# GpSimd left with the gathers alone, one-hot rows gated per token on VectorE, and a queue mark moved with each weighing

## The chip, the core and the metric

The kernel runs on one core of a Trainium2 chip. The time is the device time of one execution in microseconds (us), from the first instruction to the last, with the launch around it. Three runs of the kernel before gave 4369.52, 4371.93 and 4373.88 us; the median is 4371.93 us.

A core has five engines that run side by side, each with a queue of its own that is worked off strictly in order: PE (TensorE, matrix products), DVE (VectorE, elementwise and reductions), ACT (ScalarE, activations), POOL (GpSimd) and SP (SyncE, which here only issues DMA transfers). An instruction that waits for another engine holds up everything behind it in its own queue.

## The reference, cut to what matters

The network is a token mixer on 512 tokens, a PEER layer, and two transformer blocks with sparse attention and an MLP. The change lies in the PEER layer (`peer_ffn`), a mixture of 16384 tiny experts:

```python
q = einsum('pd,de->pe', tb, wq).reshape(-1, 8, 2, 128)
s = einsum('phik,hink->phin', q, subkeys)            # 8 heads, 2 halves, 128 keys
s1, i1 = top_k(s[:, :, 0], 16); s2, i2 = top_k(s[:, :, 1], 16)
cand = s1[..., :, None] + s2[..., None, :]           # 16 x 16 candidates
top_s, pos = top_k(cand, 16)
idx  = take_along_axis(i1 * 128 + i2, pos)           # 128 experts per token
gate = softmax(top_s)
act  = gelu(einsum('pd,phkd->phk', tb, table_u[idx]))
out  = einsum('phk,phkd->pd', gate * act, table_v[idx])
```

Each of the 512 tokens picks 128 experts (8 heads times 16), takes a dot product with a row of `peer_u` for each, and sums rows of `peer_v` weighted by gate times activation.

## The kernel before, in words

Everything is float32. A product is made of three matmuls (`mm3`, L160 to L162) on a high and a low part of each operand; `split` (L136, L137) makes the parts, the high one with a copy on ACT and the low one with a subtraction, on DVE unless another engine is named.

The first 128 tokens take the **sparse** way (`peer_few`): for each of the 128 slots a GpSimd indirect DMA (L1371) gathers one row of 1024 numbers of `peer_u` for every token into a buffer `row` (four of them), and DVE takes the dot product with the tokens (`dot`, at most three behind the gather). Then the same with `peer_v` (`axpy`). That makes 256 gathers of 512 KB.

The other 384 tokens take the **dense** way: all 16384 experts are computed, in 32 groups of 512, and a matrix of gates that is mostly zero picks what counts. The work runs in these stages:

- **Route** (`peer_route`): sixteen blocks of queries, with top-16 searches on DVE; for thirteen of them the low part of the weights is made on GpSimd (the last argument on L1166). Then, for each block of 128 tokens, **gates** (`peer_gates`): the second search, and the lookup of the chosen keys by comparing with an index row (`eq`), a multiplication on GpSimd (L1228) and a sum on DVE (L1229). Three transposes of the result on PE (L1241) end a block.
- **Spread** (`peer_spread`): for 96 quads of tokens two sets of one-hot rows are built, 128 wide each: `two` (which second key) and `one` (which first key, times the gate). GpSimd subtracts (L1259), DVE compares (L1260, L1261), PE multiplies the two (L1264), ACT copies the product to `gt`, and the gates go to DRAM (`g_dram`).
- Beside both runs `spill`: PE computes the activations of the first 18 groups (`NSPILL`) ahead of time, and SP stores them in DRAM (`a_dram`). How often it moves is set by ticks in `peer_route` and by `SR` in the spread. The sparse way moves by `FR`: 0.4 of a gather per tick of the last three gates blocks, 0.05 per quad.
- **Rounds**: for 31 groups `prepare` loads the gates and the stored activations of the next group and weighs them (`peer_weigh`: a DVE product L1312, then the split), while `peer_out` loads 2 MB of `peer_v`, splits it (`wl`, L137) and multiplies (72 matmuls of 512 columns per group on the first 17, summed in PSUM). The sparse way moves three gathers per round in the first 17 rounds and twelve after them (`QUOTA`).

The order on each engine is laid down when the program is built: a scheduler issues what it takes to be ready first. `queued(mark, ...)` only adds that an instruction on DVE may not be issued before the marked one. Every `dot` and `axpy` is queued behind `s.mark`. In route and spread the mark moves with each split of a table (L1294); in the rounds it moves where a sum is drained (L1347, L1349), and that happens first at group 16.

Of the kernel before, what the change touches and what calls it, by code (L numbers as in the profile page):

```python
# [15 lines left out]
OP = mybir.AluOpType  # L16
# [27 lines left out]
QN = (6, 5)  # L44
QUOTA = (3, 12)
YR = (0.3, 1.75)
FR = (0.4, 0.05)
SR = 0.67
FL = 3
GB = 2  # L50
# [50 lines left out]
class K:  # L101
# [1030 lines left out]
    def peer_route(s, tk, u2):  # L1132

        nc, I = s.nc, s.I
        skT = tk.tile([128, 16, 128], F32, name="skT")
        sk = I["peer_subkeys"][0].rearrange("h i n k -> n (h i) k")
        for a in range(2):
            wf = s.wp.tile([128, 1024], F32, name="wf", bufs=s.wfb)  # L1140
            f = wf.rearrange("p (a k) -> p a k", a=8)
            nc.sync.dma_start(f, sk[:, 8 * a:8 * a + 8])
            for b in range(2):
                p = s.ps()
                for c in range(4):
                    nc.tensor.transpose(p[:, 128 * c:128 * c + 128], f[:, 4 * b + c], s.ident)
                nc.scalar.activation(skT[:, 8 * a + 4 * b:8 * a + 4 * b + 4].rearrange("p a n -> p (a n)"), p, AF.Copy)
        iota = tk.tile([128, 16], F32, name="iota")
        nc.sync.dma_start(iota, s.C["iota"][:, :16])
        due = [0.0]  # L1150

        def tick(us, what=0):

            due[0] += us * YR[what > 0]
            while due[0] >= 1:
                due[0] -= 1
                yield what
        tv = s.x[:, 1].rearrange("p (b h i k) -> p b h i k", b=4, h=8, i=2)
        ti = tk.tile([128, 4, 8, 2, 16], U32, name="ti")
        lead = s.lin_lead([(I["peer_wq"][0], 0, hh) for hh in range(3)], u2, ("mm",) * 3)  # L1160
        for hh in range(16):
            if hh < 3:
                p = lead[hh]
            else:
                p = s.ps(kind="mm")
                s.lin_acc(I["peer_wq"][0], 0, hh, u2, p, nc.gpsimd)  # L1166
            q = tk.tile([128, T], F32, name="q", bufs=2)
            nc.scalar.activation(q, p, AF.Copy)
            p = s.ps()
            for tb in range(4):  # L1170
                nc.tensor.matmul(p[:, 128 * tb:128 * tb + 128], q[:, 128 * tb:128 * tb + 128], skT[:, hh], start=True, stop=True)
            sc = tk.tile([128, T], F32, name="sc", bufs=2)
            nc.scalar.activation(sc, p, AF.Copy)
            for tb in range(4):
                s.top16(tk, tv[:, tb, hh // 2, hh % 2], ti[:, tb, hh // 2, hh % 2], sc[:, 128 * tb:128 * tb + 128], 128)
                yield from tick(1.6)
        for tb in range(4):
            yield from s.peer_gates(tk, iota, tv[:, tb], ti[:, tb], tb, lambda us: tick(us, 1 + tb))

    def peer_gates(s, tk, iota, tv, ti, tb, tick):  # L1180


        nc = s.nc
        f = tk.tile([128, 8, 2, 16], F32, name="tf")
# [35 lines left out]
        for i, af in enumerate((ab, b)):  # L1220
            e = tk.tile([128, 8, 16], F32, name="e", bufs=2)
            for a in range(0, 8, 4):
                eq = tk.tile([128, 4, 16, 16], F32, name="eq", bufs=2)
                s.queued(s.mark, nc.vector.tensor_tensor, eq.rearrange("p h j a -> p (h j) a"),
                         af[:, a:a + 4].rearrange("p h j -> p (h j)")[:, :, None].to_broadcast([128, 64, 16]),
                         iota[:, None, :].to_broadcast([128, 64, 16]), op=OP.is_equal)
                yield from tick(1.2)
                nc.gpsimd.tensor_mul(eq, eq, f[:, a:a + 4, i][:, :, None, :].to_broadcast([128, 4, 16, 16]))  # L1228
                nc.vector.reduce_sum(e[:, a:a + 4].rearrange("p h j -> p (h j)"), eq.rearrange("p h j a -> p (h j) a"), axis=AX.X)  # L1229
                yield from tick(1.2)  # L1230
            es.append(e)
# [6 lines left out]
        else:  # L1238
            p = s.ps(384)
# [5 lines left out]
    def peer_spread(s, gk):  # L1245


        nc = s.nc
        iota = gk.tile([128, 128], F32, name="iota")
        nc.sync.dma_start(iota, s.C["iota"])  # L1250
        for n in range(12):
            tb, gts = n // 4, [gk.tile([128, 64, 32], F32, name="gt", bufs=3) for _ in range(2)]
            for q in range(8):
                t = 32 * (n % 4) + 4 * q
                two = gk.tile([128, 4, 128], F32, name="two", bufs=3)
                one = gk.tile([128, 4, 128], F32, name="one", bufs=3)
                i1, i2, w = (s.iT[:, tb, i, t:t + 4][:, :, None].to_broadcast([128, 4, 128]) for i in range(3))
                io = iota[:, None, :].to_broadcast([128, 4, 128])
                nc.gpsimd.tensor_sub(one, io, i1)  # L1259
                nc.vector.tensor_tensor(two, io, i2, op=OP.is_equal)  # L1260
                nc.vector.scalar_tensor_tensor(one, one, 0.0, w, op0=OP.is_equal, op1=OP.mult)  # L1261
                p = s.ps()
                for k in range(4):
                    nc.tensor.matmul(p[:, 128 * k:128 * k + 128], two[:, k], one[:, k], start=True, stop=True)  # L1264
                p3 = p.rearrange("p (t i) -> p i t", t=4)
                for half in range(2):
                    nc.scalar.activation(gts[half][:, :, 4 * q:4 * q + 4], p3[:, 64 * half:64 * half + 64], AF.Copy)
                yield
            for half in range(2):
                nc.sync.dma_start(s.g_dram[half][n], gts[half])  # L1270
# [38 lines left out]
    def peer_weigh(s, ath, atl, i, a, g):  # L1309

        a3 = a.rearrange("p (n t) -> p n t", n=12)
        s.nc.vector.tensor_mul(a3, a3, g)  # L1312
        s.split(ath[:, i], atl[:, i], a)

    def peer_values(s, grp, half, pool=None):

# [89 lines left out]
    def peer_base(s, pool, g2, tb):  # L1406

        nc = s.nc
        x1 = pool.tile([128, 1024], F32, name="row", bufs=RB)
        nc.scalar.dma_start(x1, s.x_dram[128 * tb:128 * tb + 128])  # L1410
        x = s.x[:, tb]
        nc.gpsimd.tensor_mul(x, s.acc[:, tb], g2)
        nc.vector.scalar_tensor_tensor(x, x1, ALPHA, x, op0=OP.mult, op1=OP.add)

    def peer(s, right, u2, ns, ready):
# [57 lines left out]
        with tc.tile_pool(name="vp", bufs=1, reuse_waits="tile") as vp, ExitStack() as last:  # L1473
            tabs = {}

            def prepare(grp, at):

                at += [vp.tile([128, 4, 384], F32R, name=n, bufs=2) for n in ("ath", "atl")]
                got = []
                for i in range(4):  # L1480
                    if i == 0:
                        g = vp.tile([128, 12, 4, 32], F32, name="g", bufs=GB)
# [7 lines left out]
                        nc.sync.dma_start(a, s.a_dram[grp, i])  # L1490
                        got.append((i, a, g[:, :, i]))
                    if len(got) > SKEW:
                        s.peer_weigh(*at, *got.pop(0))
                    yield
                nt = iter(())
                if ns <= grp + 1 < 32:
# [1 line left out]
                while True:  # L1498
# [1 line left out]
                    for _ in range(2):  # L1500
                        more += next(nt, s) is not s
                    if got:
                        s.peer_weigh(*at, *got.pop(0))
                    elif not more:
                        return
                    yield

            at = []
# [731 lines left out]
```

## Time and profile before

| | |
|---|---|
| median of 3 runs | 4371.93 us |
| the profiled execution | 4374.11 us, its span 4372.3 us |
| PE busy | 4131.6 us (94%) |
| DVE busy | 2938.6 us (67%) |
| ACT busy | 1781.4 us (41%) |
| POOL busy | 737.2 us (17%) |
| mean granted clock of PE | 0.976 |

The shares are means over stages that differ. The PEER layer lies between about 1440 and 2960 us. Busy time of an engine is time in which it had an instruction under way; two that follow each other overlap by some 0.08 us in the records, so that the step from start to start is the better price. [...]

### The profile page before, as it was taken

How to read it: one execution, taken by the hardware profiler on the slowest of the kernel's cores; microseconds unless marked ns; L12 is line 12 of the kernel's file. 1: busy time of each engine (PE TensorE's matmuls, PEld its weight loads, DVE VectorE, ACT ScalarE, POOL GpSimd, SP SyncE). 2: the span in 40 equal slices, each digit the busy share in tenths (PEclk: the TensorE clock that was granted, in tenths of full speed). 3: DMA queues.
4: the chain of work that ended last, by engine and by line, in shares of the span. 5: the costliest groups of instructions: out<-in, count | busy, mean ns of one | idle time of the engine just before them, and what ended most of it. 6: DMA issues, size and time to landing. Idle time of an engine off the chain costs nothing. (4 is left out here: it accounts for less than half of the span.)

```text
span 4372.3 us, 58220 instructions
## 1 busy us (share of the span) xinstructions
PE 4131.6 (94%) x21689; PEld 3483.0 (80%) x21689; DVE 2938.6 (67%) x5968; ACT 1781.4 (41%) x3262; POOL 737.2 (17%) x730
## 2 busy tenths in 40 slices
PE   7999999999999998888899999999999999899999
PEld 5888877787787898787688888887788877678887
DVE  3888887787346678997755888884652357854334
ACT  3556544444334332343233333335643234563332
POOL 0000000000000224554300433311111121311111
PEclk9999999999999999999899999999999999999999
DMA  6322311211444357646976888842123332113332
GB/s 181 91 66 87 90 44 53 63 54 51 140 142 140 109 174 249 217 183 248 320 246 224 295 299 301 301 156 82 49 78 96 96 101 70 38 49 93 96 97 92
DMA packets 474265, 607.98 MB, mean 139 GB/s; under 512 B 28127, under 2 KB 330614, under 8 KB 470910
## 3 DMA queue, kind: packets, MB, share of 16 engines
q1 hardware_dynamic: 429438, 453.18, 32.8%
q0 software_dynamic: 36864, 134.23, 8.6%
q10 hardware_dynamic: 7680, 16.85, 1.1%
q8 instruction: 171, 2.80, 0.3%
q14 instruction: 112, 0.92, 0.1%
HBM read 550.17 MB, written 54.01 MB: 138 GB/s over the span
## 5 line engine op out<-in xcount | busy, mean ns | idle before, releaser
L137 DVE TENSOR_TENSOR wl<-wf,wh 128x1024 fp32r<-128x1024 f32 (+2 forms) x482 | 578.1, 1202 | 579.4 <-ACT wh L136 570.8
L136 ACT ACTIVATE wh<-wf 128x1024 fp32r<-128x1024 f32 (+2 forms) x495 | 513.0, 1040 | 973.9 <-PE ps_mm L161 385.9
L160 PE MATMUL ps_mm<-uh,wh 128*128 128x512 f32 (+2 forms) x1104 | 412.4, 374 | 2.1 <-ACT k L492 2.1
L161 PE MATMUL ps_mm<-ul,wh 128*128 128x512 f32 (+2 forms) x1104 | 405.2, 367 | 0.0
L162 PE MATMUL ps_mm<-uh,wl 128*128 128x512 f32 (+2 forms) x1104 | 401.2, 363 | 0.0
L160 PE MATMUL ps_mm<-u2h,uth 128*128 128x384 f32 x768 | 267.7, 349 | 0.0
L162 PE MATMUL ps_mm<-u2h,utl 128*128 128x384 f32 x768 | 260.8, 340 | 0.0
L161 PE MATMUL ps_mm<-u2l,uth 128*128 128x384 f32 x768 | 260.3, 339 | 0.0
L160 PE MATMUL ps_mm<-xch,wh 128*128 128x512 f32 (+1 forms) x688 | 257.2, 377 | 2.6 <-ACT xch L136 2.4
L161 PE MATMUL ps_mm<-xcl,wh 128*128 128x512 f32 (+1 forms) x688 | 256.8, 375 | 0.3 <-DVE xcl L137 0.3
L162 PE MATMUL ps_mm<-xch,wl 128*128 128x512 f32 (+1 forms) x688 | 256.0, 373 | 0.0
L160 PE MATMUL ps_mm<-wh,ath 128*128 128x512 f32 x564 | 228.5, 406 | 12.8 <-ACT ath L136 12.8
L1371 POOL DMA_INDIRECT row<-in_peer_u_dram,ix x128 | 161.7, 1263 | 461.3 <-DVE row L492 432.5
L161 PE MATMUL ps_mm<-wl,ath 128*128 128x512 f32 x564 | 228.1, 405 | 11.7 <-DVE wl L137 11.7
L160 PEld LDWEIGHTS ps_mm<-uh,wh 128*128 128x128 f32 (+1 forms) x1104 | 209.5, 190 | 35.6 <-issue 4.4
L161 PEld LDWEIGHTS ps_mm<-ul,wh 128*128 128x128 f32 (+1 forms) x1104 | 209.6, 190 | 33.5 <-issue 5.3
L162 PEld LDWEIGHTS ps_mm<-uh,wl 128*128 128x128 f32 (+1 forms) x1104 | 209.1, 189 | 32.4 <-issue 2.8
L162 PE MATMUL ps_mm<-wh,atl 128*128 128x512 f32 x564 | 227.3, 403 | 1.1 <-DVE atl L137 1.1
L1620 POOL TENSOR_TENSOR rl<-rl 128x512 f32<-128x512 f32 x64 | 102.0, 1593 | 697.2 <-ACT rl L1619 697.2
L137 POOL TENSOR_TENSOR wl<-wf,wh 128x1024 fp32r<-128x1024 f32 x13 | 30.9, 2379 | 1006.5 <-ACT wh L136 1006.5
L1371 POOL DMA_INDIRECT row<-in_peer_v_dram,ix x128 | 149.5, 1168 | 249.4 <-DVE x L492 230.1
L1305 ACT ACTIVATE act<-ps_mm 128x384 f32<-128x384 f32 x128 | 62.9, 492 | 308.0 <-PE ps_mm L162 282.1
(660 smaller groups left out, 10894.3 us busy)
## 6 DMA issues: line engine op xcount, KB each, us to landing
uf<-in_peer_u_dram SPq DMA_DIRECT2D x128, 512.0 KB
wf<-in_peer_v_dram SPq DMA_DIRECT2D x128, 512.0 KB
wf<-in_w_in_dram SPq DMA_DIRECT2D x104, 512.0 KB
wf<-in_w_mlp_in_dram SPq DMA_DIRECT2D x64, 512.0 KB
wf<-in_w_mlp_out_dram SPq DMA_DIRECT2D x64, 512.0 KB
wf<-in_w_ada_dram SPq DMA_DIRECT2D x48, 512.0 KB
g_dram<-gt SPq DMA_DIRECT2D x24, 1024.0 KB
g<-g_dram SPq DMA_DIRECT2D x32, 768.0 KB
```

What stands on the lines that cost most here:

```text
L136: s.nc.scalar.activation(hi, src, AF.Copy)
L137: return (eng or s.nc.vector).tensor_sub(lo, src, hi.bitcast(F32)).ins
L160: nc.tensor.matmul(ps, lh, rh, start=first, stop=False)
L161: nc.tensor.matmul(ps, lh, rl, start=False, stop=False)
L162: nc.tensor.matmul(ps, ll, rh, start=False, stop=last)
L1305: s.nc.scalar.activation(a, p, AF.Gelu)
L1371: nc.gpsimd.indirect_dma_start(out=r, out_offset=None, in_=table, in_offset=bass.IndirectOffsetOnAxis(ap=e, axis=0))
L1620: nc.gpsimd.tensor_mul(r, r, r)
```

## The change

`FR` goes from (0.4, 0.05) to (0.35, 0.1). Three pieces of arithmetic leave GpSimd for DVE: the thirteen weight splits of the route, the sixteen lookups' multiplications, and four multiplications at the end of the layer. In the spread the subtraction goes, and `one` is made by four `tensor_scalar` instructions per quad, each for one token, with the key and the gate as two per-partition scalars. In the rounds of groups 1 to 17 each weighing now moves the mark.

```diff
-FR = (0.4, 0.05)
+FR = (0.35, 0.1)
...
-                s.lin_acc(I["peer_wq"][0], 0, hh, u2, p, nc.gpsimd)
+                s.lin_acc(I["peer_wq"][0], 0, hh, u2, p)
...
-                nc.gpsimd.tensor_mul(eq, eq, f[:, a:a + 4, i][:, :, None, :].to_broadcast([128, 4, 16, 16]))
+                nc.vector.tensor_mul(eq, eq, f[:, a:a + 4, i][:, :, None, :].to_broadcast([128, 4, 16, 16]))
...
-                i1, i2, w = (s.iT[:, tb, i, t:t + 4][:, :, None].to_broadcast([128, 4, 128]) for i in range(3))
-                io = iota[:, None, :].to_broadcast([128, 4, 128])
-                nc.gpsimd.tensor_sub(one, io, i1)
-                nc.vector.tensor_tensor(two, io, i2, op=OP.is_equal)
-                nc.vector.scalar_tensor_tensor(one, one, 0.0, w, op0=OP.is_equal, op1=OP.mult)
+                nc.vector.tensor_tensor(two, iota[:, None, :].to_broadcast([128, 4, 128]),
+                                        s.iT[:, tb, 1, t:t + 4][:, :, None].to_broadcast([128, 4, 128]), op=OP.is_equal)
+                for k in range(4):
+                    i1, w = (s.iT[:, tb, i, t + k:t + k + 1] for i in (0, 2))
+                    nc.vector.tensor_scalar(one[:, k], iota, i1, w, op0=OP.is_equal, op1=OP.mult)
...
-        s.split(ath[:, i], atl[:, i], a)
+        return s.split(ath[:, i], atl[:, i], a)
...
-        nc.gpsimd.tensor_mul(x, s.acc[:, tb], g2)
+        nc.vector.tensor_mul(x, s.acc[:, tb], g2)
...
+                def weigh(at, got):
+                    ins = s.peer_weigh(*at, *got.pop(0))
+                    if 0 < grp < ns:
+                        s.mark = ins
...
-                        s.peer_weigh(*at, *got.pop(0))
+                        weigh(at, got)
...
-                        s.peer_weigh(*at, *got.pop(0))
+                        weigh(at, got)
```

What this does to the queue of DVE shows at three places. First the middle of the spread, three quads. Before:

```order
L1260 TENSOR_TENSOR two<-iota,x 128x512
L1261 SCALAR_TENSOR_TENSOR one<-one,x 128x512
L1260 TENSOR_TENSOR two<-iota,x 128x512
L1261 SCALAR_TENSOR_TENSOR one<-one,x 128x512
L1260 TENSOR_TENSOR two<-iota,x 128x512
L1261 SCALAR_TENSOR_TENSOR one<-one,x 128x512
```

Of the changed kernel, the same place on DVE (the lines of the file have moved by a few):

```order
L1257 TENSOR_TENSOR two<-iota,x 128x512
L1261 TENSOR_SCALAR one<-iota,x 128x128 x4
L1257 TENSOR_TENSOR two<-iota,x 128x512
L1261 TENSOR_SCALAR one<-iota,x 128x128 x4
L1257 TENSOR_TENSOR two<-iota,x 128x512
L1261 TENSOR_SCALAR one<-iota,x 128x128 x4
```

A quad is five DVE instructions where it was two on DVE and one on GpSimd.

Second, DVE from the end of the spread to the first weighing of the rounds (`row,few_a<-row,u2t` is a dot of the sparse way, `utl` a split of the last table, `act<-act,g` the weighing). Before:

```order
L137 TENSOR_TENSOR utl<-ps_aux,uth 128x2x256 x8
L492 SCALAR_TENSOR_TENSOR row,few_a<-row,u2t 128x1024 x3
L137 TENSOR_TENSOR wl<-wf,wh 128x1024 x3
L492 SCALAR_TENSOR_TENSOR row,few_a<-row,u2t 128x1024 x4
L137 TENSOR_TENSOR wl<-wf,wh 128x1024
L492 SCALAR_TENSOR_TENSOR row,few_a<-row,u2t 128x1024 x8
L1312 TENSOR_TENSOR act<-act,g 128x384
```

Of the changed kernel, the same stretch of DVE:

```order
L137 TENSOR_TENSOR utl<-ps_aux,uth 128x2x256
L137 TENSOR_TENSOR wl<-wf,wh 128x1024
L137 TENSOR_TENSOR utl<-ps_aux,uth 128x2x256 x3
L137 TENSOR_TENSOR wl<-wf,wh 128x1024 x2
L137 TENSOR_TENSOR utl<-ps_aux,uth 128x2x256 x4
L492 SCALAR_TENSOR_TENSOR row,few_a<-row,u2t 128x1024
L137 TENSOR_TENSOR wl<-wf,wh 128x1024
L1312 TENSOR_TENSOR act<-act,g 128x384 x2
```

Fifteen dots stood ahead of the first weighing, and one stands there now.

Third, one round of DVE out of the later ones of the first 17. Before, the eleven rounds from the seventh on hold no dot:

```order
L1312 TENSOR_TENSOR act<-act,g 128x384 x3
L137 TENSOR_TENSOR wl<-wf,wh 128x1024
L1312 TENSOR_TENSOR act<-act,g 128x384
L137 TENSOR_TENSOR wl<-wf,wh 128x1024 x2
L137 TENSOR_TENSOR atl<-act,ath 128x384
L137 TENSOR_TENSOR wl<-wf,wh 128x1024
L137 TENSOR_TENSOR atl<-act,ath 128x384 x3
```

Of the changed kernel, every one of these rounds on DVE:

```order
L1312 TENSOR_TENSOR act<-act,g 128x384 x2
L137 TENSOR_TENSOR wl<-wf,wh 128x1024 x2
L1312 TENSOR_TENSOR act<-act,g 128x384 x2
L137 TENSOR_TENSOR wl<-wf,wh 128x1024
L137 TENSOR_TENSOR atl<-act,ath 128x384
L137 TENSOR_TENSOR wl<-wf,wh 128x1024
L137 TENSOR_TENSOR atl<-act,ath 128x384
L492 SCALAR_TENSOR_TENSOR row,few_a<-row,u2t 128x1024
L137 TENSOR_TENSOR atl<-act,ath 128x384 x2
L492 SCALAR_TENSOR_TENSOR row,few_a<-row,u2t 128x1024 x2
```

Three dots now stand in each round, where five to fifteen stood in each of the first six and none in the eleven after them. On PE the order changes as well: between the first and the last product of the spread stand 144 triples of activation matmuls of 384 columns where 119 stood, and after it 32 where 62 stood.

## Rows read from the trace of the kernel before

**Rows 1.** Windows: us; busy PE, PEld, DVE, ACT, POOL; PE clock, DMA share, GB/s.

```profile
1440.00:1640.00 200.00, 195.48 (x1118) 176.95 (x1116) 151.18 (x716) 66.24 (x112) 43.27 (x23) 1.00 0.40 132
1640.00:1812.00 172.00, 146.51 (x880) 141.78 (x881) 154.51 (x335) 50.07 (x91) 88.58 (x59) 0.94 0.73 251
1812.00:2028.00 216.00, 183.11 (x1262) 170.57 (x1261) 210.43 (x233) 87.96 (x239) 126.83 (x99) 0.96 0.46 175
2028.00:2080.00 52.00, 38.50 (x217) 35.66 (x215) 30.63 (x48) 13.43 (x23) 18.70 (x16) 0.87 0.97 348
2080.00:2200.00 120.00, 107.53 (x415) 84.68 (x416) 86.50 (x140) 34.13 (x47) 42.12 (x32) 0.90 0.95 324
2200.00:2380.00 180.00, 180.00 (x773) 144.77 (x773) 97.73 (x134) 64.78 (x88) 0.94 (x1) 1.00 0.70 221
2400.00:2700.00 300.00, 298.17 (x1603) 268.52 (x1602) 252.96 (x324) 98.36 (x161) 115.28 (x96) 1.00 0.86 299
```

**Rows 2.** Waits of PE, 1640 to 1812: for whom, us, times, longest.

```profile
PE ps_aux L1241 <- DVE e L1229: 15.6, 2, 8.1
```

**Rows 3.** Waits of PE, 1812 to 2028.

```profile
PE ps_aux L1264 <- DVE one L1261: 31.0, 38, 2.9
```

**Rows 4.** Waits of PE, 2028 to 2080.

```profile
PE ps_mm L160 <- ACT ath L136: 12.8, 1, 12.8
```

**Rows 5.** Waits of PE, 2080 to 2200.

```profile
PE ps_mm L161 <- DVE wl L137: 11.7, 3, 4.0
```

**Rows 6.** Groups of POOL, whole span: busy us, mean ns, idle before.

```profile
L1259 POOL TENSOR_TENSOR one<-iota,x 128x512 f32<-128x512 f32 x96 | 123.5, 1294 | 71.5 <-PE ps_aux L1264 69.5 <-DVE one L1261 1.2 <-DVE two L1260 0.6
L1228 POOL TENSOR_TENSOR eq<-eq,tf 128x1024 f32<-128x1024 f32 x16 | 40.3, 2517 | 78.8 <-DVE eq L492 78.7
```

**Rows 7.** Groups of DVE, 1640 to 1812.

```profile
L492 DVE SCALAR_TENSOR_TENSOR row<-row,u2t 128x1024 f32<-128x1024 f32 x45 | 68.2, 1519 | 0.0
...
L492 DVE TENSOR_TENSOR eq<-af,iota 128x1024 f32<-128x1024 f32 x6 | 11.7, 1944 | 0.0
```

**Rows 8.** Groups of DVE, 1812 to 2028.

```profile
L1260 DVE TENSOR_TENSOR two<-iota,x 128x512 f32<-128x512 f32 x96 | 116.2, 1212 | 0.8 <-PE ps_aux L1264 0.8
L1261 DVE SCALAR_TENSOR_TENSOR one<-one,x 128x512 f32<-128x512 f32 x96 | 83.3, 870 | 1.9 <-POOL one L1259 1.9
```

**Rows 9.** Timeline of POOL from 1904: start us, us, instruction.

```profile
1905.68 2.79 POOL L1259 TENSOR_TENSOR one<-iota,x 128x512 f32<-128x512 f32 x2 [3.12 <-PE ps_aux L1264]
```

**Rows 10.** Timeline of DVE, the same time.

```profile
1907.50 1.52 DVE L1261 SCALAR_TENSOR_TENSOR one<-one,x 128x512 f32<-128x512 f32 x1
1908.95 0.68 DVE L1260 TENSOR_TENSOR two<-iota,x 128x512 f32<-128x512 f32 x1
1909.55 0.68 DVE L1261 SCALAR_TENSOR_TENSOR one<-one,x 128x512 f32<-128x512 f32 x1
```

**Rows 11.** Timeline of DVE from 1655, in a gates block.

```profile
1655.74 1.22 DVE L492 SCALAR_TENSOR_TENSOR row<-row,u2t 128x1024 f32<-128x1024 f32 x1
...
1656.89 3.41 DVE L492 TENSOR_TENSOR eq<-af,iota 128x1024 f32<-128x1024 f32 x1
```

**Rows 12.** Groups of DVE, whole span: tensor_scalar with two or one scalars per partition.

```profile
L483 DVE TENSOR_SCALAR k<-k,noml,oml 128x768 f32<-128x768 f32 x16 | 10.7, 667 | 4.6 <-ACT E L492 4.6
L927 DVE TENSOR_SCALAR y<-y,rs 128x256 f32<-128x256 f32 x32 | 9.1, 350 | 0.3
...
L2079 DVE TENSOR_SCALAR e<-e,sm 128x128 f32<-128x128 f32 x16 | 4.6, 285 | 0.1
```

**Rows 13.** Timeline of DVE from 2036: the first weighing.

```profile
2075.01 0.55 DVE L1312 TENSOR_TENSOR act<-act,g 128x384 f32<-128x384 f32 x1
```

**Rows 14.** Timeline of SP from 2015: the first load of stored activations.

```profile
2065.68 0.32 SPq L1490 DMA_DIRECT2D act<-a_dram  x1
```

**Rows 15.** Waits of all engines, 2040 to 2200.

```profile
DVE act L1312 <- DMA act<-a_dram: 24.0, 8, 6.9
...
DVE row L492 <- DMA row<-in_peer_u_dram,ix: 13.0, 13, 1.9
```

## The prediction

> **What bounds the kernel now.** I read the windows first, stage by stage, since the busy share of the whole span (PE 94%) hides where the rest is lost [rows 1]. While the queries are routed (1440 to 1640) PE is full and DVE has 49 of 200 us free. From 1640 to 2200 it is otherwise. In the gates blocks (1640 to 1812) PE is busy 146.5 of 172 us at a mean clock of 0.94, so 138 us of full-speed work take 172: 34 lost. In the spread (1812 to 2028) it is 183.1 at 0.96, or 176 of 216: 40 lost, and DVE is busy 210.4, which is 97%. At the change of stage (2028 to 2080) 18 of 52 are lost, in the first rounds (2080 to 2200) 23 of 120. From 2200 to 2380, the same rounds without gathers, PE is full at clock 1.00.
>
> Then the waits of PE: 15.6 us for the looked-up keys `e` in the gates [rows 2], 31.0 for `one` in the spread [rows 3], 12.8 for the first weighed activations [rows 4], 11.7 for splits of `peer_v` in the first rounds [rows 5]. Three of the four name DVE; behind the third stands DVE too, as its queue shows below.
>
> The timelines say why DVE is late. A comparison or product of 512 columns takes 0.68 us, 0.60 from start to start, but 1.52 while GpSimd runs its subtraction [rows 9, 10]. The means over 96 are 1.212 and 0.870 [rows 8]. A comparison of 1024 columns, 1.22 alone, takes 3.41 beside a GpSimd multiplication of 2.5 us [rows 6, 11], and a dot averages 1.519 in the gates [rows 7]. GpSimd's tensor work is thus paid on DVE almost in full.
>
> [...] The trace agrees in size: 1.52 less 0.68 is 0.84, about what was left of a 1.3 us subtraction. [...]
>
> **Part by part.** *Gates.* DVE loses the contention: 45 dots by 0.30 are 13.5 us, 6 comparisons by 0.72 are 4.3 [rows 7, 11]. It gains 12 of the 16 multiplications by 1.15 (start to start in rows 11), 13.8. The lower rate takes 0.05 of a gather from each of about 135 ticks (`tick` adds up to 25.7 by 1.75 in each of three blocks), some 6 of these dots in this window, 7 us. That is 11 less, 143 us against PE's 138. A lookup's chain gets shorter, since 2.5 us on GpSimd become 1.15 [rows 6]. So PE's 15.6 us should about halve, and with it go some 6 of the 9 us that the clock costs: I take 14. The bounds are the whole 34, and 5 lost if the multiplications queue behind splits.
>
> *The thirteen weight splits* add 13 by 1.15 or 15 us to DVE before 1640. The 49 free us hide them, and PE waits for nothing there: 0. Without that cover they would cost up to 15. The four multiplications at the end of the layer are of the same size and replace longer ones: 0, within 3 either way.
>
> *Spread.* Before, from start to start, 96 quads of 1.212 + 0.870 - 0.16 make 184.5 us of DVE [rows 8]. Now a quad is 0.60 for `two`, as the contention is gone, and four `tensor_scalar` of 128 columns with two scalars, a form that the trace lacks. With one scalar 128 columns take 0.285 us and 256 take 0.350, so 768 would take 0.61; with two scalars 768 take 0.667 [rows 12]. The second scalar then costs 0.057, and one instruction 0.342, or 0.26 from start to start with the 0.08 by which the records overlap. The bounds are 0.20 (the second scalar costs nothing) and 0.34 (no overlap). I take 0.26, because rows 12 price each piece: a quad is 0.60 + 1.04 = 1.64, 96 are 157, 27 less. Four or five more dots by 1.15 give 5 back. DVE goes from 210 to about 188. PE's own work there is 176 plus 25 triples that the new order moves in; a 512-column matmul takes 180/773 = 0.233 us [rows 1], so one of 384 takes 0.175 and 75 take 13: 189. Two engines of 188 and 189 that wait for each other in order don't run at 100%. I take 199 for the 216, so 17, and the 13 that were moved are gone from the stage behind: 30. At 0.20 PE alone bounds the stretch, at about 193: 36. At 0.34 DVE has 219 and needs 226 at its 97%: 3.
>
> [...]
>
> *Change of stage.* Fifteen dots stand ahead of the first weighing in DVE's queue. The load of its operand is issued at 2065.68, the weighing starts at 2075.01 [rows 13, 14], and between them dots wait for their gathers, 13.0 us in 13 waits [rows 15], with the DMA engines 97% busy [rows 1]. With one dot there, what is late next is the load itself: SP issues it behind the last store of the spill, and such loads have kept DVE up to 6.9 us [rows 15]. Activation, load, weighing and split make 7 to 9, so the 12.8 shrink by some 4, with 1 of clock: 5. Bounds 0 and 12.
>
> *Rounds.* A mark in every round spreads 51 dots over 17 rounds. Ahead of the `wl` splits there are no longer 7 to 15 dots, and the 23 us lost from 2080 to 2200 can come back. But the eleven rounds that ran without gathers get three each. A round is 72 matmuls or 16.8 us; three gathers of 0.524 MB add 94 GB/s to 221, so 315. The trace has 299 GB/s with PE losing 0.6%, and 324 with PE losing 10% [rows 1]. That second row holds the bunches of dots too, and 348 GB/s were moved just before, so I take 4% of 286 us, 11, and 4 of clock: 8 gained. The bounds are 21 gained (0.6%) and 32 lost (10% with the clock of 0.90).
>
> *Sum:* 14 + 0 + 30 + 5 + 8 = 57. The profiled execution took 4374.1, so 4317; it lies 2.2 above the median of the runs, so I say 4316.
>
> **Rivals.** *The gathers fill the DMA engines in all 17 rounds.* For it: 315 lies nearer 324 than 299. Read on a straight line it loses 7% or 20 us, and 20 more at a lower clock. Against it: 348 GB/s between. The rounds then lose 17 where I have them gain 8: 32 in all, 4342.
>
> *The narrow instructions are dear.* For it: the form is not in the trace. Against it: one scalar less costs 0.285. The spread gains 3 instead of 30: 4344.
>
> *Gathers are held up by the narrow instructions.* DVE runs them for 1.04 of 1.64 us. Nine dots fall into the spread; at the longest wait for a row so far, 1.9 us [rows 15], that is 17 us of a full engine: 4334. [...] Against it: only nine gathers, ordered well ahead.
>
> *Slower: DVE queues behind late gathers in every round.* The dots now stand among the splits of each round, in order. DVE is busy 97.7 of 180 us without them [rows 1], so 7.7 of 16.8 us are free; three dots take 3.5, and 4.2 remain. From a mean wait of 1.4 us per dot on, each further us is late three times a round. At 2.5 us that is 3.3 by 17, 56 us, and with the clock near 0.90 another 29: the rounds lose 62 more than before, against 49 gained elsewhere, 4387. Against it: a mean wait of 1.0 us in the worst stretch so far [rows 15].
>
> *The change does not reach the end.* The order of PE is fixed when the program is built; if it waits elsewhere for what DVE now gives sooner, only the change of stage is left: 5, 4369. Against it: 97% of DVE in the spread.
>
> **Chances.** The forecast with its own range of 4290 to 4338 has 0.58, the full DMA engines 0.14, the dear instructions 0.12, the held gathers 0.04, no effect 0.07, slower 0.05. The range of 4274 to 4364 takes in the first four and the better bounds of gates, spread and rounds together. A measurement here tells a change from none at about 0.2%, or 9 us: faster 0.86, the same 0.08, slower 0.06.
>
> **What would show it.** Comparisons of 512 columns at 0.68 throughout and dots at 1.22. A `tensor_scalar` of the spread near 0.34 us and 0.26 apart; above 0.34 apart the spread gains nothing. The spread near 199 us, PE's wait for `e` near 8, the hole at the change of stage near 8. In the 17 rounds about 315 GB/s with PE above 95%. Wrong would be: rounds longer than 17.9 us (the full DMA engines), or dots that wait for rows in all of them.

## The result, and the profile after

The changed kernel takes 4273.26 us (median of four runs, 4272.51 to 4276.68), the kernel before on the same chip 4370.73. The ratio on record is 0.9772, with a 95% interval of 0.976 to 0.9785 (the two medians give 0.9777): 97 us less. The forecast was 4316 with a range of 4274 to 4364. The sign was right, and so were all the places but one and, in the main, the mechanism; the gain was 1.7 times what was forecast, and the time lies just outside the range.

The profiled execution has a span of 4270.9 us against 4372.3, and a mean clock of 0.985 against 0.976. To say where the 101 us between the two spans went I cut both traces at the same instructions: the last transpose of the routed queries, the first and the last matmul of the spread (L1264), the first matmul of the rounds that uses `ath`, the first sum that is drained (group 16), and the first matmul of the layer behind.

| stage, us | before | after | gained | forecast |
|---|---|---|---|---|
| up to the end of the routing | 1544.5 | 1543.7 | 0.8 | 0 |
| gates | 270.6 | 247.7 | 22.9 | 14 |
| spread | 212.0 | 186.0 | 26.0 | 17 |
| change of stage | 49.1 | 27.8 | 21.3 | 5 + 13 moved out of it |
| the 17 rounds | 297.5 | 273.8 | 23.7 | 8 |
| late rounds, end of the layer | 564.4 | 556.3 | 8.1 | 0, within 3 |
| rest | 1434.2 | 1435.6 | -1.4 | 0 |

(The rounds are counted up to the first drained sum, which comes early in the seventeenth.) Every stage that was given a gain gained more than that. Windows of the changed kernel; the columns are those of [rows 1], and the stretches are the same stages at their new times:

```profile
1440.00:1640.00 200.00, 197.09 (x1130) 178.72 (x1129) 165.40 (x741) 66.88 (x113) 8.66 (x9) 1.00 0.40 131
1640.00:1790.00 150.00, 143.89 (x900) 139.71 (x898) 138.87 (x335) 50.88 (x92) 48.83 (x39) 1.00 0.81 269
1791.00:1977.00 186.00, 181.34 (x1319) 173.46 (x1320) 185.12 (x527) 89.08 (x242) 9.71 (x9) 1.00 0.59 217
1977.00:2005.00 28.00, 20.74 (x130) 19.81 (x128) 11.73 (x17) 7.57 (x16) 0.94 (x1) 0.95 0.89 299
2005.00:2100.00 95.00, 94.77 (x399) 76.20 (x400) 72.19 (x114) 34.77 (x50) 23.13 (x18) 0.98 0.99 330
2100.00:2200.00 100.00, 100.00 (x430) 80.47 (x429) 71.09 (x108) 34.94 (x48) 26.44 (x18) 1.00 0.95 312
2200.00:2280.00 80.00, 80.00 (x344) 64.36 (x344) 54.79 (x81) 28.74 (x40) 17.60 (x13) 1.00 0.93 303
```

Read the clock column first: what was 0.94, 0.96, 0.87 and 0.90 in [rows 1] is 1.00, 1.00, 0.95 and 0.98. With PE's waits gone, most of the stretches at a lower clock went with them (in the kernel before it is 0.50 from 2070 to 2080). Then PE: 143.89 of 150 us in the gates, 181.34 of 186 in the spread, 274.77 of 275 in the rounds. DVE is busy 185.12 of 186 us in the spread: it still bounds that stage, now with next to nothing between its instructions.

The waits of PE by stage, changed kernel: the gates (1640 to 1790), the spread (1791 to 1977) and the change of stage (from 1977), against [rows 2 to 4], the longest one of each:

```profile
PE ps_aux L1291 <- DMA uf<-in_peer_u_dram: 5.4, 6, 1.7
...
PE ps_aux L1264 <- DVE one L1261: 4.3, 6, 2.1
...
PE ps_mm L160 <- ACT ath L136: 7.5, 1, 7.5
```

The wait for `e` is gone, not halved; that for `one` fell from 31.0 to 4.3; the hole at the change of stage is 7.5, inside the 7 to 9 that were worked out. From 2005 to 2280 PE has that last wait and no other: the 11.7 us for `wl` [rows 5] have no successor.

The groups of DVE that answer to [rows 6 to 8, 12], changed kernel: dots and comparisons of the gates (1640 to 1790), then the spread, then the lookups' multiplications over the whole span. Busy us, mean ns, idle before:

```profile
L492 DVE SCALAR_TENSOR_TENSOR row<-row,u2t 128x1024 f32<-128x1024 f32 x39 | 47.2, 1210 | 0.0
L492 DVE TENSOR_TENSOR eq<-af,iota 128x1024 f32<-128x1024 f32 x6 | 7.3, 1213 | 0.0
...
L1261 DVE TENSOR_SCALAR one<-iota,x 128x128 f32<-128x128 f32 x384 | 107.3, 338 | 0.0
L1257 DVE TENSOR_TENSOR two<-iota,x 128x512 f32<-128x512 f32 x95 | 64.6, 680 | 0.0
...
L1228 DVE TENSOR_TENSOR eq<-eq,tf 128x1024 f32<-128x1024 f32 x16 | 19.4, 1214 | 0.0
```

None of these is drawn out any more: dots 1.210 for 1.519, comparisons 1.213 for 1.944, `two` 0.680 for 1.212. A multiplication of the lookup takes 1.214 us on DVE where GpSimd needed 2.517. The new `tensor_scalar` takes 0.338 us, where 0.342 had been priced. The timeline of DVE inside the spread (start, us) shows its step:

```profile
1900.44 0.68 DVE L1257 TENSOR_TENSOR two<-iota,x 128x512 f32<-128x512 f32 x1
1901.04 1.11 DVE L1261 TENSOR_SCALAR one<-iota,x 128x128 f32<-128x128 f32 x4
1902.07 0.68 DVE L1257 TENSOR_TENSOR two<-iota,x 128x512 f32<-128x512 f32 x1
```

Four narrow ones run from 1901.04 and the next instruction starts at 1902.07: 0.26 each, the value taken. A quad is 1.63 us; 1.64 had been worked out.

### The profile page after: what moved, and what is told of

It reads as the page before. It is cut to its first block, busy times and chain, and to the rows that moved or that the text cites. A ratio compares the mean times of both kernels' runs of the same rounds, so it can differ in the third digit from the quotient of the medians.

```text
span 4270.9 us, 58171 instructions
## 1 busy us (share of the span) xinstructions
PE 4100.3 (96%) x21689; PEld 3461.8 (81%) x21689; DVE 2915.8 (68%) x6289; ACT 1779.5 (42%) x3262; POOL 534.2 (13%) x601
## 5 line engine op out<-in xcount | busy, mean ns | idle before, releaser
L137 DVE TENSOR_TENSOR wl<-wf,wh 128x1024 fp32r<-128x1024 f32 (+2 forms) x495 | 592.0, 1199 | 603.1 <-ACT wh L136 595.1
L1305 ACT ACTIVATE act<-ps_mm 128x384 f32<-128x384 f32 x128 | 63.2, 494 | 307.2 <-PE ps_mm L162 303.9
L492 DVE SCALAR_TENSOR_TENSOR x<-row,few_a,x 128x1024 f32<-128x1024 f32 x127 | 162.4, 1278 | 5.9 <-DMA row<-in_peer_v_dram,ix 5.9
```

What stands on the lines that cost most here:

```text
L137: return (eng or s.nc.vector).tensor_sub(lo, src, hi.bitcast(F32)).ins
L492: return fn(*args, **kw).ins
L1305: s.nc.scalar.activation(a, p, AF.Gelu)
```

## The experiments

Each starts from the changed kernel unless it says otherwise, and the diff is against it. The kernel before took 4376.81, 4373.47 and 4374.62 us beside the three sets of four experiments (medians of seven, one and nine runs), so ratios, and times of stages, compare better than times do.

**The queue mark alone taken back.** The weighings of the first groups move no mark, so gathers and dots go where the scheduler likes.

```diff
-                    if 0 < grp < ns:
-                        s.mark = ins
```

> The changed kernel (4273 us) without the mark in the rounds, all else kept. Theory A (bunched dots starve the splits of peer_v; evenly spread gathers at 315 GB/s cost PE nothing): the dots bunch again into the first seven rounds, PE waits for wl splits there, the stretch from the first to the last of the 17 rounds goes from 274 back to about 295 us, and the total is 4273 + 20 to 26 = 4293 to 4299. Theory B (the rounds gained because GpSimd's and DVE's work before them was eased, and because the clock came into them at 1.00): the rounds stay near 276 us and the total within 5 us of 4273.

Measured: 4307.96 us, ratio to before 0.9842 (0.9826 to 0.9859). Gates 248.6, spread 187.6, change of stage 32.7, rounds 303.9, late 558.5. The whole loss lies in the rounds and just ahead of them: 30.1 and 4.9. The window of the rounds, mark taken back:

```profile
2012.00:2316.00 304.00, 284.43 (x1168) 225.32 (x1168) 190.11 (x285) 97.30 (x134) 50.69 (x40) 0.96 0.84 277
```

and PE's largest wait in it:

```profile
PE ps_mm L161 <- DVE wl L137: 16.6, 5, 5.1
```

PE is busy 284 of 304 us at a clock of 0.96: it waits for `wl` splits again. The timeline of DVE ahead of the longest of these waits (PE goes on at 2119.87) shows why:

```profile
2114.69 0.56 DVE L1312 TENSOR_TENSOR act<-act,g 128x384 f32<-128x384 f32 x1 [5.80 <-DMA act<-a_dram]
2115.16 1.22 DVE L492 SCALAR_TENSOR_TENSOR row<-row,u2t 128x1024 f32<-128x1024 f32 x1
...
2116.31 1.22 DVE L1312 TENSOR_TENSOR act<-act,g 128x384 f32<-128x384 f32 x2
2117.45 1.22 DVE L492 SCALAR_TENSOR_TENSOR row<-row,u2t 128x1024 f32<-128x1024 f32 x1
...
2118.59 2.35 DVE L137 TENSOR_TENSOR wl<-wf,wh 128x1024 fp32r<-128x1024 f32 x2
```

A weighing at the head of DVE's queue waits 5.80 us for its stored activations; behind it stand two dots, two more weighings and only then the split that PE needs. The kernel before shows the same ahead of each of the three waits of [rows 5]: DVE idle for 3.1 to 5.5 us, then weighings, two dots and the split. The profile names a load for the longest of these idle times and nothing for the other two:

```profile
2178.27 0.56 DVE L1312 TENSOR_TENSOR act<-act,g 128x384 f32<-128x384 f32 x1 [5.53 <-DMA act<-a_dram]
```

So the two dots cost 2.3 us each time and the late load more. Why that load is late while the gathers come in bunches, no run here separates.

**The mark alone, put into the kernel before.**

```diff
-        s.split(ath[:, i], atl[:, i], a)
+        return s.split(ath[:, i], atl[:, i], a)
...
+                def weigh(at, got):
+                    ins = s.peer_weigh(*at, *got.pop(0))
+                    if 0 < grp < ns:
+                        s.mark = ins
```

(against the kernel before; the two calls of `s.peer_weigh` become `weigh(at, got)`)

> The kernel before with the queue mark moved per weighing and nothing else. Theory A (bunched gathers cost the rounds, and the mark alone spaces them): gates and spread stay at the times of before, about 270 and 212; the change of stage falls by 5 to 10 from 49; the rounds go from 297.5 to about 274; total about 4340 to 4348. Rival B (the rounds also need the gathers that are made early, so the mark alone is not enough): rounds stay above 290 and the total is above 4360.

Measured: 4344.24 us in one run, 30 below before. Gates 270.8 and spread 211.2 as before, change of stage 37.3 (11.8 less), rounds 275.7 (21.8 less). The rounds from 2066, mark alone:

```profile
2066.00:2342.00 276.00, 273.99 (x1166) 220.03 (x1167) 197.78 (x300) 98.41 (x136) 66.16 (x47) 0.99 0.95 310
```

PE is full at 310 GB/s. For the rounds the mark is enough by itself; it needs nothing of the rest. Put in alone it brings 30; taken back it costs 35 by the stages and some 30 by the ratios. Its share of the 97 is about a third.

**The spread's old arithmetic back** (GpSimd subtracts, two DVE instructions per quad):

```diff
-                nc.vector.tensor_tensor(two, iota[:, None, :].to_broadcast([128, 4, 128]),
-                                        s.iT[:, tb, 1, t:t + 4][:, :, None].to_broadcast([128, 4, 128]), op=OP.is_equal)
-                for k in range(4):
-                    i1, w = (s.iT[:, tb, i, t + k:t + k + 1] for i in (0, 2))
-                    nc.vector.tensor_scalar(one[:, k], iota, i1, w, op0=OP.is_equal, op1=OP.mult)
+                i1, i2, w = (s.iT[:, tb, i, t:t + 4][:, :, None].to_broadcast([128, 4, 128]) for i in range(3))
+                io = iota[:, None, :].to_broadcast([128, 4, 128])
+                nc.gpsimd.tensor_sub(one, io, i1)
+                nc.vector.tensor_tensor(two, io, i2, op=OP.is_equal)
+                nc.vector.scalar_tensor_tensor(one, one, 0.0, w, op0=OP.is_equal, op1=OP.mult)
```

> The changed kernel with the spread as it was before (subtraction on GpSimd, two wide instructions on DVE). Theory A (DVE is held while GpSimd's tensor work runs, and DVE bounds the spread): comparisons are at 1.2 us on average again, the spread takes 210 to 216 us against 186, less the 10 to 13 us of activation matmuls that move: total 4273 + 25 to 38 = 4298 to 4311. Theory B (the gain in the spread came from the lookups and splits before it, which left less for it): the spread stays below 195 us and the total below 4283.

Measured: 4314.85 us, ratio 0.9859 (0.9843 to 0.9876). Spread 213.7, change of stage 37.3, gates 254.6, rounds 274.4. The window of the spread with the old arithmetic:

```profile
1800.00:2009.00 209.00, 167.96 (x1147) 152.32 (x1147) 203.85 (x232) 81.04 (x225) 136.73 (x100) 0.96 0.50 185
```

and PE's wait in it:

```profile
PE ps_aux L1264 <- DVE one L1261: 39.1, 50, 3.1
```

Its groups of DVE in the same window:

```profile
L1260 DVE TENSOR_TENSOR two<-iota,x 128x512 f32<-128x512 f32 x92 | 107.9, 1174 | 1.2 <-PE ps_aux L1264 1.2
L1261 DVE SCALAR_TENSOR_TENSOR one<-one,x 128x512 f32<-128x512 f32 x92 | 78.4, 853 | 1.9 <-POOL one L1259 1.9
```

All of [rows 3, 8] is back: the wait, the long comparisons and the clock of 0.96, with 1147 matmuls in the stretch for 1319. The order laid down for PE puts the rest ahead (7 us in the gates) and behind (9.5 at the change of stage), so the edit is worth 27.7 in its own stage and some 40 in all (38 by the ratios, 42 by the times).

**GpSimd or the narrow form?** Two causes could hide in that: the contention, and the new form of instruction. This kernel keeps the old arithmetic but makes the subtraction on DVE, three wide instructions per quad:

```diff
+                nc.vector.tensor_sub(one, io, i1)
+                nc.vector.tensor_tensor(two, io, i2, op=OP.is_equal)
+                nc.vector.scalar_tensor_tensor(one, one, 0.0, w, op0=OP.is_equal, op1=OP.mult)
```

> The changed kernel with the spread on DVE alone but in three wide instructions per quad (subtract, compare, compare and multiply) in place of one wide and four narrow: 3 by 0.60 = 1.80 us per quad against 0.60 + 4 by 0.255 = 1.62. DVE then asks for 96 by 1.80 + 31 = 204 us in the spread. Theory A (DVE and PE each run full in this stretch, nothing is lost between them): spread 202 to 206 us, the change of stage 3 to 8 us shorter or longer as matmuls move; total 4271 + 8 to 18. Theory B (some 5% are lost wherever one of them is the bound, and the 186 us of the changed kernel were PE's own): 210 us or more.

Measured in one run: 4292.44 us, spread 204.3. The window of the spread, three wide instructions:

```profile
1793.00:1997.00 204.00, 186.98 (x1314) 176.57 (x1315) 201.84 (x334) 90.09 (x242) 10.13 (x9) 0.97 0.53 196
```

and PE's wait in it:

```profile
PE ps_aux L1264 <- DVE one L1261: 18.3, 25, 1.8
```

Of the 27.7 us between the old arithmetic (213.7) and the new (186.0), 9.4 come from taking the work off GpSimd, even though DVE then makes it itself, and 18.3 from the form that does it in fewer busy ns per quad. The two stretches don't hold the same work of PE, though (1147 matmuls with the old arithmetic, 1314 here); over the whole kernel the two parts come to about 19 us each by the ratios, the wide kernel's from its one run. The stage lasts as long as DVE needs (201.84 of 204 busy), and PE waits for it 25 times, 18.3 us in all.

**The lookups' multiplications back on GpSimd:**

```diff
-                nc.vector.tensor_mul(eq, eq, f[:, a:a + 4, i][:, :, None, :].to_broadcast([128, 4, 16, 16]))
+                nc.gpsimd.tensor_mul(eq, eq, f[:, a:a + 4, i][:, :, None, :].to_broadcast([128, 4, 16, 16]))
```

> The changed kernel with the lookups' sixteen multiplications back on GpSimd. Theory A: comparisons and dots beside them take 2 us longer in each of 16 cases, PE waits for the keys e again (15 us) and its clock falls below 1.00 in the gates blocks; 1640 to the first spread matmul takes 15 to 22 us longer, total 4288 to 4295. Theory B (PE's wait came from the fuller queue of dots, which the lower rate alone took away): within 4 us of 4273.

Measured: 4290.23 us, ratio 0.9804 (0.9788 to 0.9821); gates 266.4, all else as in the changed kernel. In the gates with this edit PE waits for `e` as in [rows 2]:

```profile
PE ps_aux L1241 <- DVE e L1229: 16.4, 3, 6.9
```

and the groups of DVE show dots and comparisons as long as in [rows 7]:

```profile
L492 DVE SCALAR_TENSOR_TENSOR row<-row,u2t 128x1024 f32<-128x1024 f32 x39 | 60.6, 1554 | 0.0
L492 DVE TENSOR_TENSOR eq<-af,iota 128x1024 f32<-128x1024 f32 x6 | 11.6, 1940 | 0.0
```

Sixteen instructions of 2.5 us, twelve of them in this stage, on an engine that is idle most of the time, cost 18.7 of the 22.9 us that the gates gained.

**The four multiplications at the end of the layer back on GpSimd:**

```diff
-        nc.vector.tensor_mul(x, s.acc[:, tb], g2)
+        nc.gpsimd.tensor_mul(x, s.acc[:, tb], g2)
```

> The changed kernel with the four multiplications at the end of the layer back on GpSimd; the prediction priced them at 0 within 3. Theory A (GpSimd's 2.4 us hold a DVE instruction each and delay utl splits that PE waits for, and its clock falls behind the wait): the stretch from the first drained sum to the first matmul of the next stage takes 564 instead of 556 us, total 4279 to 4283. Theory B (that stretch gained because the sparse way ended earlier against the groups): within 2 us of 4273.

Measured: 4279.87 us (4274.88 to 4286.66), ratio 0.9777 (0.9761 to 0.9794). By the total this can't be told from the changed kernel (0.976 to 0.9785). In the trace the late stage is 563.7 us, the 564.4 of before, while the eleven profiles of this study that have these multiplications on DVE lie at 555.8 to 560.0. The kernel with the mark alone, which has them on GpSimd too, took 564.5. Three windows of 40 us round these instructions, of before, of the changed kernel and of this one:

```profile
2860.00:2900.00 40.00, 35.45 (x182) 32.69 (x181) 29.31 (x42) 10.97 (x20) 9.00 (x4) 0.87 0.36 117
```

```profile
2766.00:2806.00 40.00, 39.49 (x216) 35.77 (x216) 35.53 (x53) 15.84 (x27) 0.00 (x0) 1.00 0.54 178
```

```profile
2775.00:2815.00 40.00, 35.19 (x187) 32.90 (x186) 30.40 (x42) 10.91 (x21) 11.59 (x4) 0.91 0.44 156
```

PE is busy 39.5 of 40 us in the second and some 35 in the others, at a lower clock. Four instructions cost 4 to 8 us. The timelines of DVE and of POOL in the kernel before show how:

```profile
2867.90 0.15 DVE L180 SCALAR_TENSOR_TENSOR nyf<-nwf,nyf 128x1 f32<-128x1 f32 x1
2867.97 1.22 DVE L137 TENSOR_TENSOR wl<-wf,wh 128x1024 fp32r<-128x1024 f32 x1
2869.11 2.35 DVE L176 SCALAR_TENSOR_TENSOR nwf<-nyf,nvf 128x1 f32<-128x1 f32 x1
```

```profile
2868.06 3.37 POOL L1412 TENSOR_TENSOR x<-x,row 128x1024 f32<-128x1024 f32 x1 [7.18 <-DVE nyf L180]
```

An instruction on one column, 0.2 us elsewhere, takes 2.35 us and ends at 2871.46 as the multiplication on GpSimd does (2871.43). What stands behind it in DVE's queue waits too, and PE with it; its waits in that window of the kernel before:

```profile
PE ps_aux L1291 <- DVE utl L137: 4.6, 3, 2.8
```

**The thirteen weight splits back on GpSimd:**

```diff
-                s.lin_acc(I["peer_wq"][0], 0, hh, u2, p)
+                s.lin_acc(I["peer_wq"][0], 0, hh, u2, p, nc.gpsimd)
```

> The changed kernel with the thirteen weight splits of the route back on GpSimd; the prediction priced them at 0. Theory A: the searches beside them have one tensor operand and are not held, PE is full before 1545 either way: stages within 1.5 us of the changed kernel, total 4268 to 4276. Theory B (GpSimd's 2.4 us hold the table splits and dots beside them): route and gates 3 to 10 us longer.

Measured in one run: 4271.39 us, no stage of the layer off by more than 1. Nothing, as priced: from 1440 to 1545 PE waits for DVE neither in the kernel before nor in the changed one. Beside GpSimd's splits, 2.38 us each, the searches from 1430 to 1560 average 0.276 to 0.285 us and the splits `utl` of 512 columns 0.677, within 0.001 of the changed kernel: none of them is drawn out.

**Four gathers a round instead of three, and six:**

```diff
-QUOTA = (3, 12)
+QUOTA = (4, 12)
```

> The changed kernel with four gathers instead of three in each of the first 17 rounds: 221 + 126 = 347 GB/s asked for. Theory A (the DMA engines carry what is asked, and PE loses nothing until they are full at about 353 GB/s): the 17 rounds stay at 274 to 280 us. Theory B (the price that the prediction took: loss grows from 299 GB/s on, and 315 only happened to be mild): 274 + 15 to 30 us. In both the later rounds stay at 556 within 3, since they are bound by PE.

```diff
-QUOTA = (3, 12)
+QUOTA = (6, 12)
```

> The changed kernel with six gathers in each of the first 17 rounds: 409 GB/s asked for, 6.81 MB per round. Theory A (full at about 353 GB/s): a round takes 6.81 / 0.353 = 19.3 us, the 17 take about 328 us against 274, DMA share at 1.0 and PE waiting for splits of peer_v. Theory B (as above, loss by a few per cent only): 290 to 305 us.

Measured, one run each: 4269.24 and 4300.08 us; rounds 274.4 and 298.6. The rounds with four gathers:

```profile
2003.00:2278.00 275.00, 275.00 (x1173) 221.10 (x1174) 216.36 (x333) 98.58 (x135) 94.99 (x64) 0.99 1.01 345
```

and with six, in three pieces:

```profile
2010.00:2100.00 90.00, 88.28 (x375) 69.95 (x374) 75.88 (x120) 29.39 (x40) 35.60 (x30) 1.00 1.05 371
2100.00:2200.00 100.00, 96.04 (x399) 75.40 (x399) 86.95 (x135) 33.33 (x46) 40.28 (x34) 0.98 1.06 378
2200.00:2300.00 100.00, 94.11 (x396) 73.48 (x395) 82.82 (x109) 32.44 (x44) 43.88 (x32) 1.00 1.04 373
```

At 345 GB/s PE is full; at 371 to 378 it loses 2 to 6% of each piece while it runs, and its rounds get longer (some 7 of their 25 us are 30 matmuls more that this kernel does before its first drained sum). So the loss of 10% at 324 GB/s in [rows 1] was not a limit of the DMA engines. With six, where PE does lose, the loss was a good deal less than the 328 us that the first theory had for the rounds: it had taken 353 GB/s, which the changed kernel moved from 2020 to 2040 at a share of 1.01, as the most that the engines carry, and they carried 373 on average.

**The shares of early gathers.** The old ones back, and then fewer than ever, none in the spread, with four per round to make up:

```diff
-FR = (0.35, 0.1)
+FR = (0.4, 0.05)
```

> The changed kernel with the old shares of early gathers (0.4 and 0.05 instead of the new ones). Theory A (VectorE's demand sets the spread): spread about 5 shorter, the gates as much VectorE time longer but with TensorE not held, so total within 4 of 4273. Rival B (more gathers early is where the spread's gain came from): spread back above 195, total above 4283.

```diff
-QUOTA = (3, 12)
+QUOTA = (4, 12)
-FR = (0.35, 0.1)
+FR = (0.3, 0.0)
```

> The changed kernel with only the first 30% of the blocks' gathers tied to the gates, none to the spread, and 4 per round in the early rounds: VectorE has no gated rows left to make in the spread. Theory A (the spread runs at VectorE's demand until TensorE's own time is the bound): spread 186 to about 181, gates 1 to 4 shorter, rounds unchanged at 274; total about 4262 to 4268 beside 4273 of the changed kernel. Rival B (TensorE's own time bounds the spread already, or the work comes back in the rounds): total within 2 of the changed kernel, or slower.

The measure beside them, the changed kernel once more:

> The changed kernel once more, unaltered, as the measure for the runs beside it on the same chip. Every theory: 4273 within 4, stages as before (gates 248, spread 186, rounds 274).

Measured: the changed kernel 4277.44 us (4273.77 to 4279.88, five runs; 0.9776 of before, 0.9762 to 0.9789), with stages as the first time (gates 248.2, spread 187.6, rounds 274.8). The old shares 4279.32 in one run: spread 180.4, gates 253.5. The new values of `FR` only move some 6 us from one stage to the next; one run shows no gain in the total. No dots in the spread: 4266.52 us (4259.68 to 4271.10, five runs; 0.9751 of before, 0.9738 to 0.9765), each of the five below each of the five beside it. That is 0.26% less than the changed kernel and the fastest version here. Its spread:

```profile
1792.00:1968.00 176.00, 175.94 (x1301) 169.17 (x1300) 173.46 (x505) 85.31 (x238) 0.00 (x0) 1.00 0.54 201
```

The spread fell to 176.1, below the 181 that was expected as PE's own time. PE is full here, so 176 is the bound that PE sets, and DVE's 173.46 hide behind it. The changed kernel put more dots into the one stage that DVE bounds. Against the run beside it that is 11.5 us of the spread, and 3.7 of them come back at the change of stage.

## Why the prediction was right, and where it was wrong

**Right.** GpSimd's tensor work was paid on DVE, and DVE set the pace in the gates and the spread. This is shown from both sides: putting sixteen multiplications back lengthens dots that have nothing to do with them from 1.210 to 1.554, and taking the subtraction to DVE shortens the spread although DVE has more to do. The price of the new form (0.26 apart), the quad (1.64 forecast, 1.63 measured), DVE's total in the spread (188, 185), the hole at the change of stage (7 to 9, 7.5), the splits at nothing, and the lookups' move from 2.5 to 1.21 us busy were all met. Too strong was "almost in full": in [rows 6, 8] comparisons drawn out from 0.68 cost DVE 69 us beside 123.5 us of subtractions, and with the twelve multiplications back (30 us) the dots and comparisons shown lose 18. A good half was paid.

**Wrong: the margins on top of the sums of work.** Three steps each took a clean sum of work and added a loss that wasn't there: 199 us for a spread that ran at 186, half of a wait in the gates that went whole, and 15 us in rounds that lost next to none. The spread fell below even its better bound (193), the rounds gained more than theirs (23.7 for 21), and so did the end of the layer (8.1 for 3); that took the time under 4274. Beside this the last step of the sum is off by 1: 4374.1 less 57 less 2.2 is 4315, not 4316.

*Spread.* "Two engines of 188 and 189 that wait for each other in order don't run at 100%. I take 199 for the 216". They ran at 186: DVE is 99.5% busy in the changed kernel, 99% with three wide instructions, and PE 100% in the version without dots. The 189 was too high as well: the version without dots does 1301 matmuls in 176 us, where 176 had been taken for the 1262 of [rows 1], from busy time multiplied by the clock. What made that too long is not settled. Spread and change of stage together gained 47.3 where 35 was forecast.

*Gates.* "PE's 15.6 us should about halve, and with it go some 6 of the 9 us that the clock costs: I take 14." DVE came out at 138.87 us in 150, below the 143 that was worked out, against PE's 143.89. The wait disappears whole, and the clock is 1.00. That DVE is no longer the longer engine may be why, or that a lookup's chain is shorter; no run separates the two. Nine us were missed by halving what should have been struck out.

*Rounds.* "I take 4% of 286 us, 11, and 4 of clock: 8 gained." PE lost 0.23 of 275 us at 315 GB/s, and nothing at 345. This is the largest miss, 15.7 us. The prediction had the reason in hand: it said that the row with 324 GB/s and 10% loss "holds the bunches of dots too", and then took a value between that row and the clean one. The mark put alone into the kernel before settles it: the loss in [rows 1] went with the bunches, whole. How the bunches cost it was only in part as predicted: ahead of each late split of [rows 5] stood not 7 to 15 dots but two, behind a weighing that waited for its load.

**Wrong: the four multiplications at the end.** "0, within 3 either way", because they are replaced by something shorter. They gained 4 to 8: the price was not the multiplication but what DVE and PE lost behind a single held instruction, and the clock after it (0.87 in that window). It is the contention that the prediction had priced elsewhere. Only the stage's time shows it; the total can't tell it.

Terms and misses add up: 8.9 in the gates, 12.3 in the spread and behind it, 15.7 in the rounds, 8.1 at the end, less 0.6 in the rest, make the 44.4 between 57 and 101.4.

**The rivals.** The full DMA engines: refuted at three gathers and at four. The dear instruction: refuted, 0.338. Late gathers that hold DVE: in the rounds DVE waits for no gather. Its two largest waits from 2005 to 2280 are for the copies of ACT ahead of the splits and for stored activations:

```profile
DVE wl L137 <- ACT wh L136: 63.4, 17, 4.8
DVE act L1312 <- DMA act<-a_dram: 10.6, 11, 3.1
```

No effect: refuted by the 97 us. Gathers held by the narrow instructions, a supposition that no row of before showed: from the same trace, the nine on GpSimd in the spread of the changed kernel against the 47 of the rounds, where DVE runs other forms:

```profile
L1371 POOL DMA_INDIRECT row<-in_peer_u_dram,ix x9 | 9.7, 1079 | 166.9 <-DVE row L492 126.5 <-DVE one L1261 40.4
```

```profile
L1371 POOL DMA_INDIRECT row<-in_peer_u_dram,ix x47 | 67.2, 1429 | 205.9 <-DVE row L492 201.6 <-DVE act L1312 4.0 <-issue 0.3
```

These means mix two cases. Three gathers of the changed kernel, and the instruction that DVE was in when each began:

```profile
1886.20 0.94 POOL L1371 DMA_INDIRECT row<-in_peer_u_dram,ix  x1 [18.82 <-DVE one L1261]
1906.41 1.15 POOL L1371 DMA_INDIRECT row<-in_peer_u_dram,ix  x1 [19.27 <-DVE row L492]
2131.37 1.68 POOL L1371 DMA_INDIRECT row<-in_peer_u_dram,ix  x1 [1.07 <-DVE row L492]
```

```profile
1885.85 0.61 DVE L1261 TENSOR_SCALAR one<-iota,x 128x128 f32<-128x128 f32 x2
1906.06 0.69 DVE L1257 TENSOR_TENSOR two<-iota,x 128x512 f32<-128x512 f32 x1
2131.02 1.22 DVE L492 SCALAR_TENSOR_TENSOR row<-row,u2t 128x1024 f32<-128x1024 f32 x1
```

Beside a narrow instruction a gather takes 0.94 us; the other two end 0.81 us after the comparison and the dot beside which they began. So gathers are held in this trace, but by DVE's long instructions with two inputs and not by the narrow ones, and nothing waits for them: DVE waits for no gather in the spread either.

## What to carry to other kernels

Before giving a small product to an idle GpSimd, look at what DVE does at that time: here a good half of it was paid on DVE, and twelve multiplications, 30 us of GpSimd, made one stage 19 us longer. When the engine that bounds a stage gets faster, add up the work of each engine without friction and take the largest: the spread and the rounds ran at that sum, the gates within some 4% of it, and the clock came back too (in the spread from 0.96 to 1.00). A row in which two causes are mixed (a transfer rate and a bunch of instructions) prices neither; take the clean row, or find a stretch with one of them alone.

## What the runs showed of the hardware

An instruction on a single column of 128 partitions took 2.35 us beside a GpSimd multiplication and 0.21 just before it, so an instruction that moves next to nothing was held too. The hold goes the other way too: in the changed kernel from 1600 to 2280 a gather that began beside a dot, a comparison, a lookup's multiplication, a weighing or a split of loaded weights ended 0.81 us or so after that instruction, 1.0 to 2.0 us in all, with few exceptions, and 0.93 to 0.94 beside a narrow instruction, a sum or a split that reads `ps_aux`. The 16 DMA engines carried 345 GB/s without PE losing anything, and 371 to 378 at a share of 1.04 to 1.06 with PE losing 2 to 6%, in one run each; the 353 that the changed kernel moved from 2020 to 2040, at a share of 1.01, had looked like the limit. A `tensor_scalar` of 128 float32 columns with two scalars per partition costs 0.338 us busy and 0.26 from start to start, against 0.285 busy with one scalar [rows 12].
